# Group 0 of a state-space mixer on one core: the first gate's GEMM ahead of the x transposes, a third convolution buffer, decay weights behind x, one decay factor by VectorE

## The chip, the core and the metric

The kernel runs on one core of one Trainium2 chip. The metric is the device time of one execution in microseconds (us). The time before is the median of three runs, 1901.63 us (1901.63, 1902.76 and 1899.21). A core has a matrix engine (TensorE, PE in the profile), a vector engine (VectorE, DVE), an activation engine (ScalarE, ACT), a general engine (GpSimd, POOL), and SyncE (SP), which here issues the DMA transfers. Each engine works through its own instructions in a fixed order and waits at an instruction whose inputs or buffers are not ready.

## What is computed

The reference is a block of two layers over 512 latent tokens and 256 context tokens of width 1024: attention and a gated FFN, then a bidirectional state-space mixer (SSD) and a gated FFN. The change concerns the mixer only. Cut to what matters:

```python
z, xbc, dt = split(h @ w_in)                 # h: latent tokens, and context tokens apart
xbc = silu(dwconv_centred(xbc, conv_w, conv_b))      # 5 taps along the tokens
x, B, C = split(xbc)                         # 8 groups of 4 heads of 64; B, C: 128 states a group
dt = softplus(dt + dt_bias)
# per direction, in chunks of 128 tokens; acs = cumsum(dt * a) within the chunk
xw     = x * exp(acs_end - acs) * dt         # "decay weights"
states = einsum(B, xw)                       # then a scan over chunks: h = h * exp(acs_end) + states
decay  = exp(where(mask, acs_q - acs_s, -inf))
y      = einsum((C B^T) * decay * dt, x) + (C h) * exp(acs)
out    = rms_norm((y_fwd + y_bwd + d_skip * x) * silu(z)) @ w_out
```

## The kernel before

**Products.** Every GEMM in fp32 is made of three products for each 128x128 weight block: high weights by high activations (L105), high weights by low activations (L106), low weights by high activations (L108). A weight panel of 128x1024 comes by DMA (`wst`, L95), ScalarE casts it to its high part `wh` (L85) and VectorE subtracts to get the low part `wl` (L87). A GEMM over the 512 latent tokens is 8 blocks by 3, so 24 products; with the context tokens 48.

**The mixer (`ssd`, from L1112).** Its 8 groups are processed one after the other. For each group `inproj` (L1257) runs six GEMMs in this order: two halves of x (`xf`), B (`Bf`), C (`Cf`), two gates (`z`). The halves of x and B need latent and context tokens, C and the gates only latent ones. Group 0's two halves of x are computed ahead, together with the norm, so group 0 begins with B and C. An x, B or C result goes through the convolution: `taken` (L1193) copies it from PSUM into one of two padded buffers `raw` on ScalarE (L1197, L1199) and multiplies the centre tap (ScalarE, L1200); `taps` (L1204) adds the other four taps on VectorE (L1205), and ScalarE applies Silu (L1209).

**The core of a group (`core`, L1284)** is a generator with steps between the GEMMs. Step 1 transposes x by 12 TensorE instructions into three PSUM banks (`ps_xt`, L1292), which ScalarE copies out (L1293). Step 2 transposes B (`ps_bt`, L1299, copied at L1300) and multiplies x by the decay weights (`xw`, L1306, VectorE). Step 3 computes C B^T (`ps_cb`, L1337), the first state (`ps_st`, L1318) and the decay matrices `E`: for each of 4 heads and 2 directions d a 128x512 tile is loaded (SP, L1350), masked (GpSimd, L1351), exponentiated by 4 ScalarE instructions (L1355) and multiplied by dt: for d=0 by 4 ScalarE instructions (L1357), for d=1 by one GpSimd instruction (L1359); VectorE adds the two (L1361). Steps 4 to 6 make the later states (VectorE adds `hs`, L1328), the outer part (`ps_yo`, L1383, scaled into `ec` at L1385) and the inner part (`ps_y`, L1392), and VectorE updates `xf` from the PSUM bank (L1395). Those later steps of a group run between the next group's x and B GEMMs, so the next group's x transposes follow right behind `ps_y` and use the PSUM banks that L1385 and L1395 set free.

**Group 0's hooks.** Inside its C GEMM run `turned` (transposes dt and the cumulative sums) and `ends` (L1230): one small matmul for the chunk ends (`ps_end`), eight ScalarE exponentials `dec` (L1238, L1239), and the decay weights `dw`: two subtractions and two multiplications by VectorE and one ScalarE exponential (L1243 to L1249).

**Order and buffers.** A scheduler turns the program into one static order for each engine; `follow` keeps ScalarE's functions in program order, since ScalarE has to load another function table (ACT_TABLE_LOAD) between Exp and Silu. PSUM has two wide buffers (tag S, for GEMMs with context, and before the change for all of them) and four banks of 128x512 (`Bank`). Behind the eight groups `ysplit` (L1429) multiplies each of the 16 gated results by a norm weight and splits them into a high part `hhy` (ScalarE, L1434) and a low part `hly` (VectorE, L1435) for the output projection (`ps_wo`); part of this already runs within group 7.

Of the kernel before, what the change touches and what calls it, by code (L numbers as in the profile page):

```python
# [7 lines left out]
P = 128  # L8
# [9 lines left out]
L = 512  # L18
# [328 lines left out]
def S(g, name):  # L347
    return g.ps.tile([P, 1024], F32, tag="S", bufs=2, name=name)
# [763 lines left out]
def ssd(g, x, norm, wf, close):  # L1112
# [17 lines left out]
    t2 = lambda nm, dt=F32, n=512: g.t3p.tile([P, n], dt, tag="t2", bufs=39, name=nm)  # L1130
    small = lambda nm, shape: g.t3p.tile(shape, F32, name=nm)
    tok = lambda t: slice(t * P + (2 if t >= 4 else 0), (t + 1) * P + (2 if t >= 4 else 0))
    def gemm(w, streams, hooks={}):
        ps = S(g, "ps_in")
        for n, _ in enumerate(gemm_in(g, [(ps, w)], h, (0, L), [[(i, 0, (L, C)[i])] for i in streams])):
            hooks.get(n, lambda: None)()
        return ps[:, :L], ps[:, L:T]


    H2 = 64  # L1140
# [41 lines left out]
            nc.sync.dma_start(dst[rows, :TH], src[H2 * d : H2 * d + 32])  # L1182
            nc.sync.dma_start(dst[rows, TH:], src[H2 * d + 32 : H2 * d + H2, : L - TH])

    raws = [small(f"raw{i}", [P, TW + 4]) for i in range(2)]
    for r in raws:
        for c0 in (0, L + 2, TW + 2):
            nc.vector.memset(r[:, c0 : c0 + 2], 0.0)
# [2 lines left out]
    late = []  # L1191

    def taken(ps, j, both, cv):  # L1193
        raw = raws[raw_n[0] % 2]
        raw_n[0] += 1
        n = TW if both else L
        nc.scalar.copy(raw[:, 2 : 2 + L], ps[0])  # L1197
        if both:
            nc.scalar.copy(raw[:, L + 4 : L + 4 + C], ps[1])  # L1199
        nc.scalar.activation(cv, raw[:, 2 : 2 + n], AF.Identity, scale=par("sw2", j), bias=par("sb", j))  # L1200
        return raw, n, j, cv
# [20 lines left out]
    def turned():  # L1222
        for src, dst in ((acs, acsT), (dt, dtT)):
            pt = Bank(g, "ps_dtT")[:, : nt * H2]
            for t in range(nt // 2):
                nc.tensor.transpose(pt[:, t * P : (t + 1) * P], src[:, t * P : (t + 1) * P], g.ident)
            nc.vector.tensor_copy(dst.rearrange("p (a c) (d h) -> p c d a h", a=2, d=2),
                                  pt.rearrange("p (c d a h) -> p c d a h", c=nt // 2, d=2, a=2))

    def ends():  # L1230
        pe = Bank(g, "ps_end")
        for d, row in ((0, P - 1), (1, 0)):
            nc.tensor.matmul(pe[:, d * nt * 32 : (d + 1) * nt * 32], g.ident[:, row : row + 1].broadcast_to([P, P]),
                             acsT[:, :, d * 32 : (d + 1) * 32], start=True, stop=True)
        pev = pe[:, : nt * H2].rearrange("p (d t h) -> p d t h", d=2, t=nt)
# [8 lines left out]
        follow(g, nc.scalar.activation(dw, dw, AF.Exp))  # L1244
# [12 lines left out]
    def inproj(gi):  # L1257

        G = Group()
        ld = lambda i: load_w(g, I["win"][6 * gi + i])  # L1260
        G.x, ahead = [], {}
        if gi == 0:
            ahead = {2: gemm(ld(2), (1, 0)), 3: gemm(ld(3), (0,), {0: turned, 5: ends})}
        for j in range(2):
            G.x.append(taps(*x0[j]) if gi == 0 else conv(gemm(ld(j), (1, 0)), 2 * gi + j, True, t3(g, "xf")))
            yield G
        for name, i, st in (("B", 2, (1, 0)), ("C", 3, (0,))):
            ps = ahead[i] if ahead else gemm(ld(i), st)
# [15 lines left out]
    def core(gi, G):  # L1284
# [59 lines left out]
        for r in range(4):  # L1344
            hd = 4 * gi + r
            E = []
            for d in range(2):
                row = d * 32 + hd
                e = t2("E")
                nc.sync.dma_start(e, ad[row : row + 1, :].broadcast_to([P, L]))  # L1350
                nc.gpsimd.affine_select(c4(e), c4(e), pattern=[[0, 4], [1 - 2 * d, P]], compare_op=ALU.is_ge,  # L1351
                                        fill=-1e30, base=0, channel_multiplier=2 * d - 1)
                for c in range(4):
                    cs = slice(c * P, (c + 1) * P)
                    follow(g, nc.scalar.activation(e[:, cs], e[:, cs], AF.Exp, bias=nacs[:, c, row : row + 1]))  # L1355
                    if d == 0:
                        nc.scalar.activation(e[:, cs], e[:, cs], AF.Identity, scale=dtT[:, c, row : row + 1])  # L1357
# [3 lines left out]
            nc.vector.tensor_tensor(E[0], E[0], E[1], ALU.add)  # L1361
            W.append(E[0])
# [334 lines left out]
```

## Time and profile before

| what | value |
| --- | --- |
| median of three runs | 1901.63 us |
| time of the profiled execution | 1901.39 us |
| its span in the trace | 1899.6 us |
| mean granted TensorE clock | 0.997 |
| the mixer's group 0, from its C GEMM to group 1's first product | 1014 to 1042 us in the span |

TensorE is busy nearly all of the time, so a change can only win where TensorE waits, and loses where it is made to wait. In the rows shown below, a timeline row gives the start and the duration in us, the engine, line and operation, the tile written and those read, the shape, how many instructions are joined in the row, and, in brackets, the idle time of the engine just before and what ended it. Durations in us are those of all the joined instructions together.

### The profile page before, as it was taken

The page shows a single profiled execution, that of the slowest core. Times are in us where ns is not written, and L with a number is a line of the kernel's source. Part 1 is how long each engine was busy: PE and PEld are TensorE (multiplying, and loading weights), DVE is VectorE, ACT ScalarE, POOL GpSimd, SP SyncE. Part 2 cuts the span into 40 slices and gives each one's busy share as a digit, 9 for nine tenths or more (in the row PEclk, how much of TensorE's full clock was granted, in tenths as well). Part 3 has the DMA queues.
Part 4 walks back from the last instruction along what each step waited for, and adds up shares of the span by engine and source line. Part 5 has one row for each costly group of instructions (what it writes and reads, how often), then busy time and mean ns, then how long its engine had stood idle before and what let it go on. Part 6 is the DMA issues. An engine that isn't in the chain of part 4 may idle for free.

```text
span 1899.6 us, 27442 instructions
## 1 busy us (share of the span) xinstructions
PE 1867.0 (98%) x10794; PEld 1532.9 (81%) x10794; DVE 1336.4 (70%) x2006; ACT 836.0 (44%) x1436; POOL 234.9 (12%) x220
## 2 busy tenths in 40 slices
PE   9999999999999999999998999999999999999999
PEld 7865545689888888888887888888888888888887
DVE  5688989678777777444477777777878576565555
ACT  3655544354222222222256677766667353323331
POOL 2100000030000000000030334443335200000000
PEclk9999999999999999999999999999999999999999
DMA  9223341024443564222223333444344323323232
GB/s 339 68 83 101 100 144 62 1 68 160 152 131 117 174 189 154 67 67 67 67 79 106 104 118 112 122 122 133 112 130 118 98 78 102 101 85 111 89 100 89
DMA packets 73489, 210.02 MB, mean 111 GB/s; under 512 B 8976, under 2 KB 14480, under 8 KB 73232
## 3 DMA queue, kind: packets, MB, share of 16 engines
q1 hardware_dynamic: 73360, 208.26, 35.0%
q8 instruction: 85, 1.39, 0.3%
q14 instruction: 44, 0.36, 0.1%
HBM read 198.79 MB, written 6.82 MB: 108 GB/s over the span
## 4 chain that ended last, share of the span: by engine, by line
PE 81%; DVE 9%; issue 3%; DMA 3%; ACT 3%; POOL 1%; SPq 0%; DVEq 0%; POOLq 0%; ACTq 0%
PE ps_up L105 10%; PE ps_up L106 10%; PE ps_up L108 10%; PE ps_d L105 6%; PE ps_d L108 5%; PE ps_d L106 5%; PE ps_in L106 4%; PE ps_in L108 4%; PE ps_in L105 4%; PE ps_o L799 2%; PE ps_s L835 2%; PE ps_st L1318 2%; PE ps_wo L108 1%; DVE wl L87 1%; PE ps_wo L105 1%
## 5 line engine op out<-in xcount | busy, mean ns | idle before, releaser
L87 DVE TENSOR_TENSOR wl<-wst,wh 128x1024 fp32r<-128x1024 f32 x211 | 263.1, 1247 | 235.4 <-PE ps_up L106 120.7
L85 ACT CAST wh<-wst 128x1024 fp32r<-128x1024 f32 x211 | 221.2, 1049 | 407.1 <-DMA wst<-in_wup 311.1
L106 PE MATMUL ps_up<-hlf,wh 128*128 128x512 f32 x992 | 351.6, 354 | 0.0
L108 PE MATMUL ps_up<-hhf,wl 128*128 128x512 f32 x992 | 351.4, 354 | 0.0
L105 PE MATMUL ps_up<-hhf,wh 128*128 128x512 f32 x992 | 351.2, 355 | 0.0
L105 PEld LDWEIGHTS ps_up<-hhf,wh 128*128 128x128 f32 x992 | 187.5, 189 | 26.2
L106 PEld LDWEIGHTS ps_up<-hlf,wh 128*128 128x128 f32 x992 | 187.6, 189 | 26.0
L108 PEld LDWEIGHTS ps_up<-hhf,wl 128*128 128x128 f32 x992 | 187.5, 189 | 26.1
L105 PE MATMUL ps_in<-hhs,wh 128*128 128x512 f32 (+1 forms) x544 | 199.2, 366 | 0.0
L106 PE MATMUL ps_in<-hls,wh 128*128 128x512 f32 (+1 forms) x544 | 193.9, 356 | 0.0
L108 PE MATMUL ps_in<-hhs,wl 128*128 128x512 f32 (+1 forms) x544 | 193.3, 355 | 0.0
L105 PE MATMUL ps_d<-hdh,wh 128*128 128x512 f32 (+1 forms) x496 | 173.4, 351 | 0.1
L108 PE MATMUL ps_d<-hdh,wl 128*128 128x512 f32 (+1 forms) x496 | 173.4, 350 | 0.0
L106 PE MATMUL ps_d<-hdl,wh 128*128 128x512 f32 (+1 forms) x496 | 172.9, 349 | 0.0
L1015 DVE SCALAR_TENSOR_TENSOR X<-ps_d,mod,X 128x256 f32<-128x256 f32 (+1 forms) x176 | 102.7, 614 | 25.7 <-PE ps_d L108 25.4
L105 PEld LDWEIGHTS ps_in<-hhs,wh 128*128 128x128 f32 x544 | 103.0, 189 | 14.6 <-issue 0.9
L108 PEld LDWEIGHTS ps_in<-hhs,wl 128*128 128x128 f32 x544 | 102.8, 189 | 14.5
L106 PEld LDWEIGHTS ps_in<-hls,wh 128*128 128x128 f32 x544 | 103.1, 189 | 12.9
L106 PEld LDWEIGHTS ps_d<-hdl,wh 128*128 128x128 f32 x496 | 93.2, 188 | 14.4 <-DVE hdl L87 0.2
L108 PEld LDWEIGHTS ps_d<-hdh,wl 128*128 128x128 f32 x496 | 93.2, 188 | 13.1
L105 PEld LDWEIGHTS ps_d<-hdh,wh 128*128 128x128 f32 x496 | 93.0, 188 | 13.1 <-ACT hdh L85 0.3
L838 ACT ACTIVATE pr<-ps_s 128x1024 f32<-128x1024 f32 x56 | 57.2, 1021 | 97.4 <-PE ps_s L837 95.4
(373 smaller groups left out, 3672.5 us busy)
## 6 DMA issues: line engine op xcount, KB each, us to landing
wst<-in_wup SPq DMA_DIRECT2D x88, 512.0 KB, 3.6
wada<-in_adaT SPq DMA_DIRECT2D x56, 512.0 KB, 3.7
wst<-in_win SPq DMA_DIRECT2D x48, 512.0 KB, 3.6
wst<-in_wdown SPq DMA_DIRECT2D x44, 512.0 KB, 3.7
E<-ad SPq DMA_DIRECT2D x64, 256.0 KB, 6.9
wada<-in_adaB SPq DMA_DIRECT2D x24, 512.0 KB, 5.0
ec<-ead SPq DMA_DIRECT2D x64, 128.0 KB, 5.2
wst<-in_wout SPq DMA_DIRECT2D x16, 512.0 KB, 3.7
```

The lines of the kernel that those rows point to most:

```text
L85: keep(nc.scalar.copy(hi, src))
L87: keep(eng.tensor_tensor(lo, src, _r(hi), ALU.subtract))
L105: mm(out, wh, ah, start=first, stop=False)
L106: mm(out, wh, al, start=False, stop=False)
L108: i = mm(out, wl, ah, start=False, stop=last)
L799: nc.tensor.matmul(po[S64[e], :n], v, pr[:, 512 * e + off : 512 * e + off + n], start=first, stop=last)
L835: nc.tensor.matmul(outs[e], a[S64[e], k], b[S64[e], q], start=i == 0, stop=False)
L838: nc.scalar.activation(pr, ps, AF.Exp)
L1015: nc.vector.scalar_tensor_tensor(ap, o[:, c0:c1], gate[:, m, v : v + 1], ap, ALU.mult, ALU.add)
L1318: nc.tensor.matmul(ps[:, d * 256 : (d + 1) * 256], Bt[:, t * P : (t + 1) * P], xw[d][t], start=t == ts[0], stop=t == ts[-1])
```

## The change

Four edits, all in `ssd`. In group 0 the B result is taken right behind its GEMM, and the first gate's GEMM (`first_z`, into a PSUM bank instead of a wide buffer) is issued behind C and ahead of the x transposes. There are three padded `raw` buffers instead of two, in all groups. The decay weights are cut out of `ends` into `weights`, called behind x's taps and Silu. In group 0 the multiplication of the d=0 decay matrices by dt is one VectorE instruction of 128x512 instead of four of ScalarE.

```diff
-    def gemm(w, streams, hooks={}):
-        ps = S(g, "ps_in")
+    def gemm(w, streams, hooks={}, make=S):
+        ps = make(g, "ps_in")
...
-        return ps[:, :L], ps[:, L:T]
+        return ps[:, :L], ps[:, L:T] if make is S else None
...
-    raws = [small(f"raw{i}", [P, TW + 4]) for i in range(2)]
+    raws = [small(f"raw{i}", [P, TW + 4]) for i in range(3)]
...
-        raw = raws[raw_n[0] % 2]
+        raw = raws[raw_n[0] % 3]
...
+    pev = []
+
     def ends():
...
         for i, (tf, tb) in enumerate(steps):
-            follow(g, nc.scalar.activation(dec[:, i, 0], pev[:, 0, tf], AF.Exp))
-            follow(g, nc.scalar.activation(dec[:, i, 1], pev[:, 1, tb], AF.Exp))
-
+            follow(g, nc.scalar.activation(dec[:, i, 0], pev[0][:, 0, tf], AF.Exp))
+            follow(g, nc.scalar.activation(dec[:, i, 1], pev[0][:, 1, tb], AF.Exp))
+
+    def weights():
         for d in range(2):
             hs = slice(d * 32, d * 32 + 32)
-            nc.vector.tensor_tensor(dw[:, :, hs], pev[:, d], acsT[:, :, hs], ALU.subtract)
+            nc.vector.tensor_tensor(dw[:, :, hs], pev[0][:, d], acsT[:, :, hs], ALU.subtract)
         follow(g, nc.scalar.activation(dw, dw, AF.Exp))
         nc.vector.tensor_tensor(dw, dw, dtT, ALU.mult)
...
-        G.x, ahead = [], {}
+        G.x = []
         if gi == 0:
-            ahead = {2: gemm(ld(2), (1, 0)), 3: gemm(ld(3), (0,), {0: turned, 5: ends})}
+            B = taken(gemm(ld(2), (1, 0)), 8 * 2, True, t3(g, "Bf"))
+            Cp = gemm(ld(3), (0,), {0: turned, 5: ends})
+            first_z = gemm(ld(4), (0,), make=Bank)
...
+            if gi == 0:
+                if i == 2:
+                    weights()
+                got = B if i == 2 else taken(Cp, 8 * i, False, t2("Cf"))
+            else:
+                ps = gemm(ld(i), st)
             yield None
-            setattr(G, name, conv(ps, 8 * i + gi, i == 2, t3(g, "Bf") if i == 2 else t2("Cf")))
+            if gi:
+                got = taken(ps, 8 * i + gi, i == 2, t3(g, "Bf") if i == 2 else t2("Cf"))
+            setattr(G, name, taps(*got))
...
-            ps = gemm(ld(4 + j), (0,))
+            ps = first_z if gi == j == 0 else gemm(ld(4 + j), (0,))
...
-                    if d == 0:
+                    if d == 0 and gi:
                         nc.scalar.activation(e[:, cs], e[:, cs], AF.Identity, scale=dtT[:, c, row : row + 1])
-                if d:
-                    nc.gpsimd.tensor_tensor(c4(e), c4(e), dtT[:, :4, row : row + 1].broadcast_to([P, 4, P]), ALU.mult)
+                if d or gi == 0:
+                    (nc.gpsimd if d else nc.vector).tensor_tensor(c4(e), c4(e), dtT[:, :4, row : row + 1].broadcast_to([P, 4, P]), ALU.mult)
```

How it moves the instructions, at three places. The first is TensorE in group 0, from the end of the C GEMM (`hls_7`, `hhs_7` are the last activation blocks of a GEMM, `hhs_0` the first): the difference between the two orders, with the 24 products of the first gate standing between its two pieces.

```order
 L106 MATMUL ps_in<-hls_7_4404,wh 128x512
 L108 MATMUL ps_in<-hhs_7_4403,wl 128x512
-L1292 MATMUL ps_xt<-cst,xf 128x128 x12
 L105 MATMUL ps_in<-hhs_0_4389,wh 128x512
...
 L108 MATMUL ps_in<-hhs_7_4403,wl 128x512
+L1305 MATMUL ps_xt<-cst,xf 128x128 x12
 L105 MATMUL ps_in<-hhs_0_4389,wh 128x512
```

The 12 x transposes stood between C and the first gate; now they stand between the first gate and the second. The B transposes, which stood 5 products into the second gate, now stand 17 products into it. On ScalarE the same stretch, from the cast of group 1's first weight panel to the Silu of B, was before:

```order
L85 CAST wh<-wst 128x1024
L1244 ACTIVATE dw<-dw 128x384
L1209 ACT_TABLE_LOAD
L1209 ACTIVATE xf<-xf 128x770 x2
L1197 COPY raw_9357<-ps_in 128x512
L1199 COPY raw_9357<-ps_in 128x256
L1197 COPY raw_9358<-ps_in 128x512
L1200 ACTIVATE Bf<-raw_9357,par 128x770
L1200 ACTIVATE Cf<-raw_9358,par 128x512
L1293 COPY xt<-ps_xt 128x512 x3
L85 CAST wh<-wst 128x1024
L1209 ACTIVATE Bf<-Bf 128x770
```

and is now:

```order
L85 CAST wh<-wst 128x1024
L1209 ACT_TABLE_LOAD
L1209 ACTIVATE xf<-xf 128x770 x2
L1247 ACT_TABLE_LOAD
L1247 ACTIVATE dw<-dw 128x384
L1197 COPY raw_9357<-ps_in 128x512
L1306 COPY xt<-ps_xt 128x512
L1200 ACTIVATE Cf<-raw_9357,par 128x512
L1306 COPY xt<-ps_xt 128x512 x2
L1209 ACT_TABLE_LOAD
L1209 ACTIVATE Bf<-Bf 128x770
```

B's copy and centre tap have moved ahead of the cast; the exponential of the decay weights has moved behind the Silu of x, between two more table loads. The second place is VectorE at the x transposes of group 3 (groups 5 and 7 read the same), around B's last tap. Before, the update of `xf` from `ps_y` came first and both `ec` behind it:

```order
L87 TENSOR_TENSOR wl<-wst,wh 128x1024
L1205 SCALAR_TENSOR_TENSOR Bf<-raw_9357,par,Bf 128x770
L1395 SCALAR_TENSOR_TENSOR xf<-xf,par,ps_y 128x512
L1385 TENSOR_TENSOR ec<-ec,ps_yo 128x512 x2
L1396 TENSOR_TENSOR xf<-xf,ec 128x512
```

Now one `ec` stands ahead of it:

```order
L87 TENSOR_TENSOR wl<-wst,wh 128x1024
L1205 SCALAR_TENSOR_TENSOR Bf<-raw_9359,par,Bf 128x770
L1398 TENSOR_TENSOR ec<-ec,ps_yo 128x512
L1408 SCALAR_TENSOR_TENSOR xf<-xf,par,ps_y 128x512
L1398 TENSOR_TENSOR ec<-ec,ps_yo 128x512
L1409 TENSOR_TENSOR xf<-xf,ec 128x512
```

On TensorE the three banks of x transposes stood there as 8, four products, 4; they now stand as 8, one product, 4, and the second bank waits for that first `ec`, the third for `xf`. The third place is ScalarE at the end of group 7, ahead of its first decay exponential (`hhy` are the high parts for the output projection). Before:

```order
L1322 COPY hs<-ps_st 128x512
L1434 ACTIVATE hhy_13650<-z,par 128x512
L85 CAST wh<-wst 128x1024
L1434 ACTIVATE hhy_13666<-z,par 128x512
L1355 ACT_TABLE_LOAD
```

Now:

```order
L1335 COPY hs<-ps_st 128x512
L1447 ACTIVATE hhy_13658<-z,par 128x512
L1447 ACTIVATE hhy_13714<-z,par 128x512
L1447 ACTIVATE hhy_13730<-z,par 128x512
L1368 ACT_TABLE_LOAD
```

Eight `hhy` stand ahead of the exponentials now, six before; the two that moved ahead had stood behind the last exponential.

More of the change, by code (lines that the diff above doesn't have):

```diff
@@ L1234, in ends @@
                              acsT[:, :, d * 32 : (d + 1) * 32], start=True, stop=True)
[L1235 removed]
+        pev.append(pe[:, : nt * H2].rearrange("p (d t h) -> p d t h", d=2, t=nt))
         for i, (tf, tb) in enumerate(steps):
[L1238 to L1239 removed]
+            follow(g, nc.scalar.activation(dec[:, i, 0], pev[0][:, 0, tf], AF.Exp))
+            follow(g, nc.scalar.activation(dec[:, i, 1], pev[0][:, 1, tb], AF.Exp))
+    def weights():
         for d in range(2):
             hs = slice(d * 32, d * 32 + 32)
[L1243 removed]
+            nc.vector.tensor_tensor(dw[:, :, hs], pev[0][:, d], acsT[:, :, hs], ALU.subtract)
         follow(g, nc.scalar.activation(dw, dw, AF.Exp))
@@ L1260, in inproj @@
         ld = lambda i: load_w(g, I["win"][6 * gi + i])
-        G.x, ahead = [], {}
+        G.x = []
         if gi == 0:
-            ahead = {2: gemm(ld(2), (1, 0)), 3: gemm(ld(3), (0,), {0: turned, 5: ends})}
+            B = taken(gemm(ld(2), (1, 0)), 8 * 2, True, t3(g, "Bf"))
+            Cp = gemm(ld(3), (0,), {0: turned, 5: ends})
+            first_z = gemm(ld(4), (0,), make=Bank)
         for j in range(2):
-            G.x.append(taps(*x0[j]) if gi == 0 else conv(gemm(ld(j), (1, 0)), 2 * gi + j, True, t3(g, "xf")))
+            G.x.append(taps(*x0[j]) if gi == 0 else
+                       conv(gemm(ld(j), (1, 0)), 2 * gi + j, True, t3(g, "xf")))
             yield G
         for name, i, st in (("B", 2, (1, 0)), ("C", 3, (0,))):
-            ps = ahead[i] if ahead else gemm(ld(i), st)
+            if gi == 0:
[4 more added lines that the diff above has]
+                ps = gemm(ld(i), st)
             yield None
-            setattr(G, name, conv(ps, 8 * i + gi, i == 2, t3(g, "Bf") if i == 2 else t2("Cf")))
+            if gi:
+                got = taken(ps, 8 * i + gi, i == 2, t3(g, "Bf") if i == 2 else t2("Cf"))
+            setattr(G, name, taps(*got))
             yield G
```

## The prediction

> **What bounds the kernel now.** I read the page first, then the list of waits, then the chain of waits and the timelines of the engines around group 0 of the mixer. The page gives the span and the busy times by engine:
>
> ```profile
> span 1899.6 us, 27442 instructions
> PE 1867.0 (98%) x10794; PEld 1532.9 (81%) x10794; DVE 1336.4 (70%) x2006; ACT 836.0 (44%) x1436; POOL 234.9 (12%) x220
> ```
>
> TensorE is idle for 1899.6 - 1867.0 = 32.6 us in all; no other engine can be the bound as a whole, so what counts is which wait of TensorE ends last at a place. The list of waits (us in total, times, longest) has the largest single one in group 0:
>
> ```profile
> PE ps_xt L1292 <- ACT xf L1209: 5.2, 1, 5.2
> PE ps_xt L1292 <- DVE xf L1395: 1.8, 6, 0.5
> ```
>
> The x transposes of group 0 wait 5.22 us for the Silu of x; in the six groups from 2 on they wait 0.3 us on average for a PSUM bank. The chain, in order of time (start, us), tells what the first wait is made of:
>
> ```profile
> 1017.53 3.96 DMA wst<-in_win
> 1021.51 1.05 ACT wh L85
> 1022.56 0.42 ACT dw L1244
> 1023.00 1.28 ACT L1209
> 1024.29 0.85 ACT xf L1209
> ```
>
> ScalarE casts a panel of group 1 that came at 1021.51, does the exponential of the decay weights, loads the Silu table and only then does the Silus. TensorE's timeline of that stretch, from the end of C to group 1's first product:
>
> ```profile
> 1025.19 2.92 PE L1292 MATMUL ps_xt<-cst,xf 128*128 128x128 f32 x12 [5.22 <-ACT xf L1209]
> 1027.77 0.67 PE L105 MATMUL ps_in<-hhs,wh 128*128 128x512 f32 x1
> ...
> 1028.50 0.39 PE L108 MATMUL ps_in<-hhs,wl 128*128 128x512 f32 x1
> ...
> 1034.42 0.39 PE L106 MATMUL ps_in<-hls,wh 128*128 128x512 f32 x1
> ...
> 1034.81 0.88 PE L1299 MATMUL ps_bt<-cst,Bf 128*128 128x128 f32 x6
> ...
> 1035.45 0.48 PE L108 MATMUL ps_in<-hhs,wl 128*128 128x512 f32 x1
> ...
> 1039.87 1.05 PE L1337 MATMUL ps_cb<-Cf,Bf 128*128 128x128 f32 x8
> ...
> 1042.30 0.47 PE L105 MATMUL ps_in<-hhs,wh 128*128 128x256 f32 x1
> ```
>
> C ends at 1025.19 - 5.22 = 1019.97, and nothing runs until 1025.19. Between 1028.50 and 1034.42 stand 26 products, 0.228 us each. The wait costs more than itself, since the clock drops. The windows (span, then PE, PEld, DVE, ACT, POOL, granted clock, DMA share, GB/s) show 0.50 right behind it:
>
> ```profile
> 1025.00:1026.00 1.00, 0.81 (x4) 0.57 (x5) 0.85 (x1) 1.00 (x3) 0.00 (x0) 0.50 0.00 0
> ```
>
> The 12 transposes take 1027.77 - 1025.19 = 2.58 us there. At full clock, in group 1, the same 12 stand in two pieces with the next product behind each:
>
> ```profile
> 1081.47 0.66 PE L1292 MATMUL ps_xt<-cst,xf 128*128 128x128 f32 x4
> 1081.88 0.47 PE L105 MATMUL ps_in<-hhs,wh 128*128 128x512 f32 x1
> ...
> 1082.66 1.20 PE L1292 MATMUL ps_xt<-cst,xf 128*128 128x128 f32 x8
> 1083.61 0.48 PE L105 MATMUL ps_in<-hhs,wh 128*128 128x512 f32 x1
> ```
>
> That is 0.41 + 0.95 = 1.36 us, so the low clock costs 1.2 us.
>
> **The gate's GEMM in the wait.** Its 24 products take 24 x 0.228 = 5.47 us, from 1019.97 to 1025.44. No work is added to TensorE. It can only start at once if its weights are there, which ScalarE's and VectorE's timelines show (casts of both gates' panels, and the low part of one):
>
> ```profile
> 1006.93 2.00 ACT L85 CAST wh<-wst 128x1024 fp32r<-128x1024 f32 x2
> 1008.01 1.23 DVE L87 TENSOR_TENSOR wl<-wst,wh 128x1024 fp32r<-128x1024 f32 x1 [0.18 <-ACT wh L85]
> ```
>
> They lie 10 us ahead. The Silu of x loses the 0.42 us of `dw` ahead of it: cast done at 1022.56, table 1.28, both Silus:
>
> ```profile
> 1024.29 1.58 ACT L1209 ACTIVATE xf<-xf 128x770 f32<-128x770 f32 x2
> 1017.84 3.81 DVE L1205 SCALAR_TENSOR_TENSOR xf<-raw,par,xf 128x770 f32<-128x770 f32 x4
> ```
>
> So x is ready at 1022.56 + 1.28 + 1.58 = 1025.42, just as the gate ends; the taps, 0.95 us each, end near 1023.6 once the decay weights' subtractions stand behind them (1021.65 and two more). The wait of 5.22 us becomes about nothing, the clock stays up, and the transposes end at 1025.44 + 1.36 = 1026.8.
>
> **What is late next.** The 17 products ahead of the B transposes end at 1026.8 + 3.9 = 1030.7. B's Silu now has this ahead of it on ScalarE from 1025.42: a table load, the `dw` exponential, C's copy, a copy of `xt`, C's centre tap, two more copies, a second table load, and its own 0.85 (as x's first Silu in the chain), by these rows:
>
> ```profile
> 1026.51 0.60 ACT L1197 COPY raw<-ps_in 128x512 f32<-128x512 f32 x1
> ...
> 1027.92 0.82 ACT L1200 ACTIVATE Cf<-raw,par 128x512 f32<-128x512 f32 x1
> 1028.63 1.56 ACT L1293 COPY xt<-ps_xt 128x512 f32<-128x512 f32 x3
> ```
>
> 1.28 + 0.42 + 0.60 + 1.56 + 0.82 + 1.28 + 0.85 = 6.8 us, less 0.1 for each of some three overlaps (1027.92 + 0.82 lies 0.11 past the next start): B is ready at 1031.9 to 1032.2, I take 1032.0. TensorE waits 1.3 us there, **a new wait**, where the row at 1034.81 shows next to none now. The bounds: nothing, if the copies overlap more, and 2.8, if C's tap or the copies wait on PSUM as well. Then 0.64 for the transposes (1034.81 to 1035.45), 7 products of 1.6, and 2.43 for `ps_cb` and `ps_st` (1039.87 to 1042.30): group 1 starts at 1036.7 instead of 1042.30. VectorE has to have the weighted x by then:
>
> ```profile
> 1029.01 0.75 DVE L1205 SCALAR_TENSOR_TENSOR Cf<-raw,par,Cf 128x512 f32<-128x512 f32 x1
> ...
> 1035.59 3.02 DVE L1306 TENSOR_TENSOR xw<-xt,dw 128x512 f32<-128x512 f32 x4
> ```
>
> From 1023.6: four taps of B (3.8), two weight subtractions (2.4 by the row at 1008.01), four of C (3.0), about 1.4 for the pieces of `dw` and its neighbours (an estimate), two of the `xw` (1.5): 1035.7, where the second product of the first state would ask for it some 0.3 us earlier. That leaves a gain of **5.3 us** in group 0.
>
> **The edits that I put at nothing.** The d=0 factor takes 16 ScalarE instructions away, and adds four by VectorE:
>
> ```profile
> 1045.19 0.68 ACT L1357 ACTIVATE E<-E,dtT 128x128 f32<-128x128 f32 x2
> 1061.33 0.69 DVE L1361 TENSOR_TENSOR E<-E 128x512 f32<-128x512 f32 x1
> ```
>
> ScalarE saves 16 x 0.29 (start to start) = 4.7 us, VectorE gains 4 x 0.6 to 1.5 us (that sum is slowed beside GpSimd elsewhere in the trace). The products that use these matrices stand behind two GEMMs of group 1, 20 us later, which hides both; with that cover gone it would cost up to 6 us. Three memsets more lie far ahead of group 0. SP now issues the eight loads of the decay matrices behind three weight panels instead of four:
>
> ```profile
> 1036.08 6.38 SPq L1350 DMA_DIRECT2D E<-ad  x8
> ```
>
> The fourth panel, one of group 1 that is wanted three GEMMs (some 30 us) later, is issued some 6 us later for it; that cover hides it, and without it those 6 us would be TensorE's.
>
> **Later groups.** The 5.3 us are a shift, unless a wait changes size. A third `raw` buffer reorders VectorE at the transposes of groups 1 to 7. The rows of group 6, with `xf` ahead of the transposes that it holds up, the second being two `ec`:
>
> ```profile
> 1358.49 0.73 DVE L1395 SCALAR_TENSOR_TENSOR xf<-xf,par,ps_y 128x512 f32<-128x512 f32 x1
> 1359.15 1.27 DVE L1385 TENSOR_TENSOR ec<-ec,ps_yo 128x512 f32<-128x512 f32 x2
> ...
> 1359.28 1.35 PE L1292 MATMUL ps_xt<-cst,xf 128*128 128x128 f32 x8 [0.46 <-DVE xf L1395]
> ```
>
> In groups 3, 5 and 7 one `ec` (0.64) now stands ahead of `xf`, against a weight subtraction less (1.2) since the first tap of x: the bounds are the present wait of 0.3 gone, and 0.6 added, in each; I take +0.2 each, **+0.6**. Group 1, without a wait now, gets the like of the others: **+0.3**. Groups 4 and 6 have their third bank wait for an `ec` alone, and their present waits (0.24 and 0.46) go: **-0.7**. In group 2 the wait for C's Silu goes, as C's taps now begin one place earlier: **-0.6**. At the end of group 7 `ps_y` already waits for a decay exponential:
>
> ```profile
> 1150.38 1.16 PE L1337 MATMUL ps_cb<-Cf,Bf 128*128 128x128 f32 x8 [0.57 <-ACT Cf L1209]
> 1445.79 1.06 PE L1392 MATMUL ps_y<-E,xt 128*64 128x128 f32 x14 [0.90 <-ACT E L1355]
> 1429.73 0.73 ACT L1434 ACTIVATE hhy<-z,par 128x512 fp32r<-128x512 f32 x1
> ```
>
> Two more `hhy` ahead of the exponentials are 2 x 0.62 (the next starts at 1430.35): **+1.2**. Bounds are nothing and 2.2.
>
> **Sum:** -5.3 + 0.6 + 0.3 - 0.7 - 0.6 + 1.2 = -4.5 us. Against the profiled execution (1901.39, of which 1899.6 span; it lies 0.24 under the median of the runs) that gives **1896.9 us**.
>
> **Rivals.** (1) *Nothing given back:* group 0 in full, the later waits of 1.8 and 0.57 gone, and the tail unchanged, because VectorE runs ahead with a third buffer: -5.3 - 2.4 = -7.7, 1893.7. For it speaks the subtraction that left the stretch, against it the rows at 1359, where VectorE works without a gap. (2) *The table switches cost more than their loads.* ScalarE would have to run empty before each; the row at 1023.00 starts 0.02 us after `dw` ends, and Silu 0.01 after the load, against it. If each of the two added switches cost another load's time, B comes 2.6 us later: -1.9, 1899.5. (The Trainium skill, "ScalarE: Activation LUTs", section "What ACT_TABLE_LOAD costs", states a drain of about 1380 ns beside each load of 1283 ns; by it the sum would be -1.7. The trace has the load at 1.28 and no such gap.) (3) *The change doesn't do what it says:* if the gate's panel were the one cast at 1021.51, TensorE would wait 3 to 4 us for it and the rest would follow: -1 to -2, 1900. The casts at 1006.93 speak against it. (4) *Slower:* VectorE late at the second bank in all seven later groups. Without the terms above, group 0 and the tail leave -4.1; a delay d each uses it up at d = 0.6 us, which is one `ec`, and one `ec` and a tap (0.64 + 0.95 = 1.6) in front of it give -4.1 + 11.2 = +7.1, 1908.5. The order has the `ec`, not the tap, and a tap less work in front.
>
> **How the numbers follow.** The forecast, give or take 1.5, has 0.45; rival 1, 0.2; rival 2, 0.1; rival 3, 0.05; a smaller form of rival 4 (0.4 to 0.7 us in each group, 1899 to 1902), 0.13; rival 4 in full, 0.07. What a measurement can tell from no change is about 0.2%, 3.8 us, so faster means below 1897.8. That is some three quarters of the forecast's case and rival 1: 0.53; slower 0.07; the same 0.40. The range reaches to rival 1 and over most of the smaller form of rival 4: 1893.6 to 1901.2.
>
> **What would show it.** No idle time of TensorE between C and the gate, a wait under 0.5 us at the x transposes with the clock at 1.00; a new wait of 1.3 us at the B transposes for ScalarE's Silu; group 1's first product near 1037.0; waits under 0.7 us at the later transposes; 2.1 us at the last `ps_y`. Wrong would be a wait for weights at the gate, a wait of several us at `ps_bt`, `ps_cb` or `ps_st`, or waits over 1 us at the later transposes.

## The result and the profile after

| | before | after |
| --- | --- | --- |
| median of 7 runs each, us | 1899.97 | 1906.87 |
| profiled execution: time, span, us | 1901.39, 1899.6 | 1906.87, 1905.1 |
| A: from `ps_end` to group 1's first product, us | 24.52 | 19.42 |
| B: from there to the start of the last `ps_y` product of group 7, us | 412.9 | 425.9 |

The ratio is 1.0034, with a 95% interval of 1.0023 to 1.0044: slower by 6.5 us by the ratio (the medians differ by 6.9), where the forecast was 4.5 us faster. The two stretches of the table say where. Group 0 won 5.1 us, where 5.3 were forecast; the seven groups behind it, whose code gives the same work, lost 13.0. (What lies ahead of A is 1.7 us shorter after, by one stretch of 3.4 us at half clock that only the trace of before has there; what lies behind B is 0.7 shorter. The start of A lay anywhere between 1014.3 and 1018.8 us in the fourteen kernels profiled here, so I compare stretches and not the span.)

The page of the kernel after, span and busy time by engine:

```profile
span 1905.1 us, 27469 instructions
PE 1868.2 (98%) x10794; PEld 1533.7 (81%) x10794; DVE 1349.4 (71%) x2013; ACT 834.8 (44%) x1422; POOL 227.3 (12%) x220
```

TensorE does the same 10794 matmuls. ScalarE has 14 instructions fewer (16 gone, two table loads come), VectorE seven more (four products, three memsets). Nothing here looks like a loss; TensorE's idle time has grown from 32.6 to 36.9 us. The list of waits of the kernel after (engine, tile, who ended the wait; us in all, times, longest) has its new entries on top:

```profile
PE ps_xt L1305 <- DVE ec L1398: 9.0, 6, 3.0
PE ps_xt L1305 <- DVE xf L1408: 1.9, 1, 1.9
...
PE ps_bt L1312 <- ACT Bf L1209: 1.2, 1, 1.2
```

The 5.2 us for the Silu of x are gone, and 1.2 us at B's transposes have come. But the later x transposes, which waited 1.8 us in all for a PSUM bank, now wait 10.9. By group, 1 to 7: 0.17, 1.90, 1.22, 1.87, 1.71, 2.98, 1.09. With the smaller waits at `ps_cb` and `ps_y` that is 12.5 us against 3.2 in stretch B, 9.2 of the 13.0 lost. Some 3.4 more is the clock behind two of those waits, by windows of the kernel after (span, then PE, PEld, DVE, ACT, POOL, granted clock, DMA share, GB/s):

```profile
1135.00:1137.00 2.00, 2.00 (x6) 1.58 (x5) 0.68 (x1) 1.01 (x2) 1.28 (x1) 0.51 0.00 0
1137.00:1139.00 2.00, 2.00 (x7) 1.56 (x6) 0.70 (x2) 1.23 (x2) 0.45 (x1) 0.64 0.00 0
...
1363.00:1365.00 2.00, 1.88 (x8) 1.59 (x9) 1.32 (x3) 2.00 (x4) 0.55 (x1) 0.68 0.00 0
1365.00:1367.00 2.00, 2.00 (x6) 1.51 (x6) 1.20 (x2) 0.34 (x1) 0.73 (x1) 0.50 0.00 0
```

Each window of 2 us loses 2 x (1 - clock): 0.98 + 0.72 behind the wait of group 2, 0.64 + 1.0 behind that of group 6 (and 0.06 in the next window, at 0.97): 1.7 us each time. In stretch B of before the clock does not fall.

**Group 0** reads as forecast. TensorE's timeline of the kernel after (start, duration, operation, shape, idle time before it):

```profile
1016.04 0.81 PE L1235 MATMUL ps_end<-acsT,cst 128*128 128x192 f32 x4
...
1023.54 1.47 PE L1305 MATMUL ps_xt<-cst,xf 128*128 128x128 f32 x12
...
1030.13 0.88 PE L1312 MATMUL ps_bt<-cst,Bf 128*128 128x128 f32 x6 [1.22 <-ACT Bf L1209]
...
1033.74 2.08 PE L1331 MATMUL ps_st<-xw,Bt 128*128 128x256 f32 x8 [0.22 <-DVE xw L1319]
1035.46 0.47 PE L105 MATMUL ps_in<-hhs,wh 128*128 128x256 f32 x1
```

The transposes have no wait in brackets and last 1.47 us where they lasted 2.92.

**Later groups.** VectorE has one long stretch of work, from the first later state (which needs the first part of `ps_st`) to the row that frees the waited bank of x transposes. TensorE's timeline of group 6, before:

```profile
1326.60 2.75 PE L1318 MATMUL ps_st<-xw,Bt 128*128 128x256 f32 x12
```

and after:

```profile
1327.46 2.75 PE L1331 MATMUL ps_st<-xw,Bt 128*128 128x256 f32 x12
...
1363.12 0.66 PE L1305 MATMUL ps_xt<-cst,xf 128*128 128x128 f32 x4 [2.98 <-DVE ec L1398]
```

Counted from the start of `ps_st`, TensorE is ready for that bank at 1359.28 - 0.46 - 1326.60 = 32.2 us before (by the row of 1359.28 in the prediction, where it is the second of the three banks) and at 1363.12 - 2.98 - 1327.46 = 32.7 after, where it is the third; it gets it at 32.7 before and 35.7 after. VectorE is 3 us late. Its stretch begins, before, with

```profile
1327.73 0.69 DVE L1328 TENSOR_TENSOR hs<-hs,ps_st 128x512 f32<-128x512 f32 x1 [8.08 <-PE ps_st L1318]
1328.34 0.68 DVE L1361 TENSOR_TENSOR E<-E 128x512 f32<-128x512 f32 x1
```

and after it begins and ends with

```profile
1327.48 1.42 DVE L87 TENSOR_TENSOR wl<-wst,wh 128x1024 fp32r<-128x1024 f32 x1 [7.10 <-PE ps_in L106]
1328.83 0.68 DVE L1341 TENSOR_TENSOR hs<-hs,ps_st 128x512 f32<-128x512 f32 x1
1331.62 1.10 DVE L1374 TENSOR_TENSOR E<-E 128x512 f32<-128x512 f32 x1 [2.12 <-POOL E L1372]
...
1362.38 0.68 DVE L1398 TENSOR_TENSOR ec<-ec,ps_yo 128x512 f32<-128x512 f32 x1
```

A weight subtraction of 1.42 us now stands ahead of the first state, and the sum of the decay matrices waits 2.12 us for GpSimd's factor, which was ready before. The decay matrices come late from their loads on. SP's loads and GpSimd's first factor for this stretch, before:

```profile
1310.08 5.75 SPq L1350 DMA_DIRECT2D E<-ad  x8
1324.11 1.05 POOL L1359 TENSOR_TENSOR E<-E,dtT 128x512 f32<-128x512 f32 x1 [0.60 <-ACT E L1355]
```

and after:

```profile
1317.12 5.68 SPq L1363 DMA_DIRECT2D E<-ad  x8
1330.55 1.05 POOL L1372 TENSOR_TENSOR E<-E,dtT 128x512 f32<-128x512 f32 x1
```

SP begins the loads 16.5 us ahead of `ps_st` before and 10.3 after, and the factor, done 1.4 us ahead of `ps_st` before, is done 4.1 behind its start. It is the same in all six stretches that end at the transposes of groups 2 to 7: the loads stand on SP behind one weight panel more than before, and that panel waits for a buffer until a GEMM ends.

The windows over the whole stretch, before:

```profile
1326.60:1359.20 32.60, 32.22 (x205) 27.93 (x203) 28.70 (x33) 20.64 (x46) 9.24 (x7) 1.00 0.26 78
1161.40:1194.10 32.70, 32.70 (x209) 28.38 (x207) 28.45 (x32) 21.22 (x47) 9.25 (x7) 1.00 0.23 67
```

and after (the first of each is group 6, the second group 3):

```profile
1327.40:1363.10 35.70, 32.74 (x209) 28.25 (x208) 31.77 (x34) 23.07 (x52) 14.87 (x13) 1.00 0.31 91
1157.50:1190.10 32.60, 31.38 (x201) 27.30 (x201) 29.57 (x33) 22.19 (x53) 13.43 (x11) 1.00 0.34 94
```

VectorE, the third busy column, is busy 28.70 of 32.60 us in group 6 before: 88%, in a kernel where its share of the span is 70%. After it needs 31.77. That is one subtraction more (34 instructions against 33) and slower ones, beside a GpSimd that has 13 instructions there in place of 7: four of its masks and the first factor, among others, now fall into the stretch. The 3.9 us of idle time are the same in sum. Group 3 is of another kind. VectorE is busier (29.57 against 28.45 in windows of nearly the same length) and yet not later, but TensorE asks earlier. TensorE's timeline before:

```profile
1161.44 2.75 PE L1318 MATMUL ps_st<-xw,Bt 128*128 128x256 f32 x12
...
1192.10 0.66 PE L1292 MATMUL ps_xt<-cst,xf 128*128 128x128 f32 x4
...
1193.52 0.60 PE L1292 MATMUL ps_xt<-cst,xf 128*128 128x128 f32 x4
1194.35 0.66 PE L1292 MATMUL ps_xt<-cst,xf 128*128 128x128 f32 x4 [0.23 <-DVE xf L1395]
```

and after:

```profile
1157.56 2.75 PE L1331 MATMUL ps_st<-xw,Bt 128*128 128x256 f32 x12
...
1190.10 0.66 PE L1305 MATMUL ps_xt<-cst,xf 128*128 128x128 f32 x4 [1.22 <-DVE ec L1398]
```

The waited bank comes free 32.9 us behind `ps_st` before and 32.5 after. TensorE asked for it at 32.7, as the third bank of its transposes; it now asks at 31.3, since it is the second. By these rows the old order of the transposes was 4, four products, 8, and not the 8, four products, 4 that the section on the change has; so the second bank, asked for at 32.1 before, is now asked for four products sooner.

How late the bank is goes by when the sum of the decay matrices can start. In groups 3, 5 and 7 of the kernel after and of two of the runs below (`e4` and `e6`), TensorE and VectorE have the same rows in the same order up to the bank. The sum starts 2.5 to 3.8 us behind `ps_st` in these nine stretches, always after a wait for GpSimd's factor, the bank comes free 29.7 to 29.8 us behind the sum, and TensorE's wait goes from 0.98 to 2.21 us with it. With one order the wait of a group thus differs by up to 1.2 us from trace to trace; smaller differences between single groups say nothing below.

### The profile page after: what moved, and what is told of

Read it like the earlier page. It is cut to its first block, busy times and chain, and to the rows that moved or that the text cites. A ratio compares the mean times of both kernels' runs of the same rounds, so it can differ in the third digit from the quotient of the medians.

```text
span 1905.1 us, 27469 instructions
## 1 busy us (share of the span) xinstructions
PE 1868.2 (98%) x10794; PEld 1533.7 (81%) x10794; DVE 1349.4 (71%) x2013; ACT 834.8 (44%) x1422; POOL 227.3 (12%) x220
## 4 chain that ended last, share of the span: by engine, by line
PE 72%; DVE 13%; issue 5%; ACT 4%; DMA 3%; POOL 2%; SPq 1%; DVEq 0%; POOLq 0%; ACTq 0%
PE ps_up L105 10%; PE ps_up L106 10%; PE ps_up L108 10%; PE ps_d L105 6%; PE ps_d L108 5%; PE ps_d L106 5%; DVE xf L1205 2%; PE ps_o L799 2%; PE ps_in L106 2%; PE ps_in L108 2%; PE ps_in L105 2%; PE ps_s L835 2%; DVE wl L87 1%; PE ps_wo L105 1%; PE ps_wo L108 1%
```

## The experiments

The theory was that VectorE's order in the later groups is what costs, and the first question which of the edits changes it, since none touches those groups but the third buffer. Rivals were that buffer, and the work that VectorE gained.

**The factor back on ScalarE** (`e1`), the rest of the change kept:

```diff
-                    if d == 0 and gi:
+                    if d == 0:
...
-                if d or gi == 0:
-                    (nc.gpsimd if d else nc.vector).tensor_tensor(c4(e), c4(e), dtT[:, :4, row : row + 1].broadcast_to([P, 4, P]), ALU.mult)
+                if d:
+                    nc.gpsimd.tensor_tensor(c4(e), c4(e), dtT[:, :4, row : row + 1].broadcast_to([P, 4, P]), ALU.mult)
```

> The changed kernel with group 0's d=0 factor back on ScalarE; gate, third buffer and split weights stay. Its order of VectorE in groups 2 to 7 is that of before again (the xf update ahead of both ec at B's last tap). Theory (the factor's move changes the scheduler's order of the later groups, and that order costs the time): the waits at the later x transposes fall from 10.9 us to about 2, group 0 keeps its gain, 1893 to 1897 us. Rival A (VectorE is the bound of groups 2 to 7 at any order, so a gain of TensorE in group 0 is given back there): 1902 to 1908. Rival B (the third buffer reorders the later groups, as the prediction had it): unchanged, 1905 to 1908.

**The factor alone** (`e2`): the kernel before, with only those lines of the change.

> The kernel of before with only the d=0 factor of group 0 moved to VectorE. Theory (order): waits of 8 to 11 us at the later x transposes where before has 1.8, 1907 to 1911 us. Rival A (TensorE arriving earlier is the cause): TensorE does not arrive earlier here, so 1899 to 1901. Rival B (third buffer): 1899 to 1901. The prediction's price for the edit itself was nothing.

**The third buffer alone** (`e3`), on the kernel before:

```diff
-    raws = [small(f"raw{i}", [P, TW + 4]) for i in range(2)]
+    raws = [small(f"raw{i}", [P, TW + 4]) for i in range(3)]
...
-        raw = raws[raw_n[0] % 2]
+        raw = raws[raw_n[0] % 3]
```

> The kernel of before with only the third raw buffer. Its order of VectorE in the later groups is that of before. Theory (order by the factor): 1899 to 1901 us, waits at the later transposes about 2. Rival B (the third buffer): 8 us slower or more, about 1908.

**The factor on GpSimd** (`e4`): the change, with the product on GpSimd in place of VectorE.

```diff
-                    (nc.gpsimd if d else nc.vector).tensor_tensor(c4(e), c4(e), dtT[:, :4, row : row + 1].broadcast_to([P, 4, P]), ALU.mult)
+                    nc.gpsimd.tensor_tensor(c4(e), c4(e), dtT[:, :4, row : row + 1].broadcast_to([P, 4, P]), ALU.mult)
```

> The changed kernel with the four d=0 factors of group 0 on GpSimd instead of VectorE: no added VectorE work, but ScalarE is as free as in the changed kernel, and the later groups have the changed kernel's order. Theory (the order, not the work of the four instructions): 1904 to 1909 us, waits at the later transposes near 10. Rival C (the four VectorE instructions push VectorE back, and it never recovers): waits near 2, 1894 to 1898.

Measured (the medians of before that the ratios go by lie between 1899.75 and 1900.9; A and B are the stretches of the table above):

| | median us | ratio to before | A | B |
| --- | --- | --- | --- | --- |
| e1, factor back | 1896.67 | 0.9985 [0.9976, 0.9994] | 19.68 | 412.9 |
| e2, factor alone | 1912.76 | 1.0066 [1.0053, 1.0078] | 25.12 | 424.5 |
| e3, buffer alone | 1892.81 | 0.9964 [0.9952, 0.9977] | 19.05 | 412.6 |
| e4, factor on GpSimd | 1908.02 | 1.0039 [1.0026, 1.0053] | 19.23 | 426.3 |

The first line of the waits at the x transposes, of e1:

```profile
PE ps_xt L1305 <- DVE xf L1408: 1.5, 6, 0.4
```

of e2:

```profile
PE ps_xt L1292 <- DVE ec L1385: 11.9, 7, 2.7
```

and of e4:

```profile
PE ps_xt L1305 <- DVE ec L1398: 10.9, 6, 2.8
```

The later loss comes and goes with the factor, by itself 11.6 us in B, more than I expected; and it stays when VectorE does not do the factor at all. So the third buffer is not its cause, and VectorE's four products are not either. What e2, e4 and the change have in common is that ScalarE no longer has those 16 instructions in group 0.

The third buffer alone was expected to change next to nothing. It made the fastest kernel of the study. Its waits at the x transposes:

```profile
PE ps_xt L1292 <- DVE xf L1395: 2.0, 6, 0.5
...
PE ps_xt L1292 <- ACT xf L1209: 0.9, 1, 0.9
```

The wait of 5.2 us has shrunk to 0.9, with the gate's code where it was. ScalarE's timeline gives the reason: in e3 B's result is copied out of its wide PSUM buffer, into the third `raw`, at

```profile
1011.70 0.57 ACT L1197 COPY raw<-ps_in 128x512 f32<-128x512 f32 x1
1012.17 0.37 ACT L1199 COPY raw<-ps_in 128x256 f32<-128x256 f32 x1
```

and in the kernel before only behind x's Silus, when x's taps had let go of a `raw`:

```profile
1025.78 0.57 ACT L1197 COPY raw<-ps_in 128x512 f32<-128x512 f32 x1
1026.25 0.37 ACT L1199 COPY raw<-ps_in 128x256 f32<-128x256 f32 x1
```

With the wide buffer free 14 us earlier, the scheduler itself puts 18 of the gate's 24 products ahead of the x transposes.

**The same work with the instructions back** (`e5`) tells apart the order and the work. ScalarE gets 16 multiplications by 1.0, in place, where its factor was; VectorE still does the factor:

```diff
                     if d == 0 and gi:
                         nc.scalar.activation(e[:, cs], e[:, cs], AF.Identity, scale=dtT[:, c, row : row + 1])
+                    elif d == 0:
+                        nc.scalar.activation(e[:, cs], e[:, cs], AF.Identity, scale=1.0)
```

> The changed kernel, with VectorE still multiplying the d=0 matrices of group 0 by dt, and 16 ScalarE instructions (a multiplication by 1.0 in place) put where before had the factor. VectorE's work is that of the changed kernel in every group; its order from group 3 on is that of before but for one row in group 6. Theory (the order alone costs the time): waits at the later x transposes about 2 us, stretch from group 1 to the last inner product as in e1 (412 us against 425 in the changed kernel), 1894 to 1899 us. Rival C (VectorE's added work): waits near 10, 1904 to 1909.

Measured: 1895.62, ratio 0.9973 [0.9963, 0.9983], B 413.5. The waits at the x transposes of e5:

```profile
PE ps_xt L1305 <- DVE xf L1410: 2.7, 6, 1.2
```

More work than the change, on VectorE the same, and 11.3 us faster. Sixteen ScalarE instructions that compute nothing bring back the old order of TensorE, GpSimd and (but for one row in group 6) VectorE in the stretches of groups 3 to 7, and with it the loads 16.5 us ahead of `ps_st`. Group 2 keeps another order, its loads begin 10.0 us ahead, and it is the one with the wait of 1.2 us. The loss is the static order that the scheduler chose.

**What in that order costs.** The second question was whether one move would mend it. The update of `xf` ahead of both `ec` (`e6`) tried the row that the transposes wait for; the weight subtractions of the gates behind the last later state (`e7`) tried the subtraction ahead of the first state; the first later state ahead of the sums of the decay matrices (`e12`) tried GpSimd's factor in front of the states.

```diff
+            pos = []
...
-                late.append(nc.vector.tensor_tensor(ec[d], ec[d], po, ALU.mult))
-            nc.gpsimd.tensor_tensor(ec[0], ec[0], ec[1], ALU.add)
+                pos.append(po)
...
+            for d in range(2):
+                late.append(nc.vector.tensor_tensor(ec[d], ec[d], pos[d], ALU.mult))
+            nc.gpsimd.tensor_tensor(ec[0], ec[0], ec[1], ALU.add)
```

> The changed kernel with the update of xf written ahead of both ec; that changes VectorE's order only at B's last tap in groups 4 and 6 (update, then both ec, as before had it there). The prediction's step (the row that frees the bank sets the wait): the waits of groups 4 and 6, 1.87 and 2.98 us now, fall to 0.2 to 0.6. Theory (what stands ahead of VectorE's stretch, from the first later state on, sets it): they stay within 0.7 us of what they are, and the time within 2 us of the changed kernel, 1905 to 1909.

`e7` (`behind` adds an order between two instructions, `last_hs` is the last later state):

```diff
-            ps = first_z if gi == j == 0 else gemm(ld(4 + j), (0,))
+            if gi:
+                wz = ld(4 + j)
+                behind(g.last_wl, last_hs[0])
+                ps = gemm(wz, (0,))
+            else:
+                ps = first_z if j == 0 else gemm(ld(4 + j), (0,))
```

> The changed kernel with the low parts of the gates' weight panels bound behind the last later state of the group before, so that none stands ahead of the first state on VectorE (one fewer there in groups 2 to 7; group 2's order becomes that of before). Theory (what stands ahead of the first later state delays the whole stretch): the wait of group 2 falls from 1.9 to about 0.2, those of groups 3 to 7 by 0.5 to 1.2 each, 1901 to 1904 us. If only the row that frees the bank matters, waits of groups 3 to 7 stay and the time is 1905 to 1907.

`e12`:

```diff
-            nc.vector.tensor_tensor(E[0], E[0], E[1], ALU.add)
-            W.append(E[0])
+            W.append(E)
...
-        for i in range(1, 4):
+        state(1, xw)
+        i1 = last_hs[0]
+        for n, E in enumerate(W):
+            behind(nc.vector.tensor_tensor(E[0], E[0], E[1], ALU.add), i1)
+            W[n] = E[0]
+        for i in range(2, 4):
```

> The changed kernel with the sums of the two decay matrices bound behind the first later state, so that VectorE no longer waits for GpSimd's factor ahead of it in groups 3, 5 and 7 (there the first later state starts 3.6 to 4.3 us behind TensorE's product now, 1.1 in groups 2, 4 and 6, whose order stays). Theory (each delay ahead of or within VectorE's stretch is passed on): in groups 3, 5 and 7 the first state starts about 1.1 us behind, and the waits there (1.22, 1.71, 1.09) fall below 0.7; those of groups 2, 4 and 6 stay between 1.3 and 3; 1902 to 1905 us. Rival (the wait for GpSimd is only moved behind the state, and the stretch ends as late): waits of groups 3, 5 and 7 stay over 1 us, 1905 to 1908.

Measured: e6 1908.37, 1.0040 [1.0026, 1.0053]; e7 1915.19, 1.0078 [1.0064, 1.0093]; e12 1912.25, 1.0066 [1.0049, 1.0083]. None mended anything, and e7 and e12 are slower than either of their expectations. In e6 the bank came with the other row and as late (waits of 2.42 and 2.19 us in groups 4 and 6). In e7 the stretch holds as many subtractions as in the change, but the one that stood at its head, while VectorE waited for GpSimd's factor anyway, now comes behind the states; the waits grew to 3.11 to 4.65 us in groups 3 to 7: a miss by sign. In e12 the first state did start 1.2 to 1.3 us behind `ps_st` in groups 3, 5 and 7, and the waits there stayed at 1.99, 1.20 and 1.40. In all three the loads of the decay matrices still begin 10 to 11 us ahead of `ps_st`, and the first sum starts 2.3 to 4.3 us behind it. That late start is common to every stretch of groups 2 to 7 with a wait of 0.98 us or more, in e2 and e4 too; in all others the loads begin 16.5 us ahead or sooner, and the wait is 0.87 or less. No run moved the loads alone, so that they are the cause within the order is read from the traces and not tested.

**Is the stretch without slack?** (`e9`) The kernel before, with one weight subtraction of 128x1024 done a second time in groups 2 to 7 (`last_st` is the staged panel):

```diff
+            wz = ld(4 + j)
+            if gi >= 2 and j:
+                nc.vector.tensor_tensor(wz[1], g.last_st, _r(wz[0]), ALU.subtract)
-            ps = gemm(ld(4 + j), (0,))
+            ps = gemm(wz, (0,))
```

> The kernel of before with one VectorE subtraction of 128x1024 (1.2 us) repeated without effect in each group from 2 on. The scheduler puts it ahead of the row that frees the bank in groups 3, 5 and 7, and behind that row in groups 2, 4 and 6. Theory (between the later states and the freed bank VectorE has no slack in any order, although it is busy 70% of the span): waits of 1.2 to 2 us at the x transposes of groups 3, 5 and 7 (0.2 to 0.4 before), and under 0.7 in groups 2, 4 and 6; 1903 to 1906 us. If VectorE had slack there: no wait over 0.6 us, 1899 to 1902 us.

Measured: 1912.01, 1.0061 [1.0048, 1.0074]. Six times 1.2 us on an engine that idles 30% of the span cost 12 us, 2 a group, more than either theory gave. The waits of e9:

```profile
PE ps_cb L1341 <- ACT Cf L1210: 9.0, 6, 2.7
...
PE ps_xt L1296 <- DVE ec L1389: 2.0, 3, 0.8
PE ps_xt L1296 <- DVE xf L1399: 1.9, 3, 0.9
```

The transposes wait 2 us more than before, `ps_cb` 8.4 more: VectorE is behind there too, with C's taps, which ScalarE's Silu and then TensorE wait for. That fits a stretch without slack, and the shortage runs on past the x transposes. But the scheduler moved other rows as well (in groups 3, 5 and 7 one `ec` stands ahead of `xf`, and the taps of C alternate with the products of the weighted x), so the 12 us are the price of the work and of these moves together.

**What the parts of the change are worth without the new order.** The gate's GEMM ahead and the third buffer, without the factor and the weights (`e8`); the gate alone (`e10`); the weights behind x alone (`e11`), each on the kernel before, with the change's own lines. For e8 the difference to the change is, beside the lines of e1:

```diff
-    def weights():
...
-                if i == 2:
-                    weights()
```

> Before with the first gate ahead of the x transposes and the third buffer; decay weights and factor as before. VectorE's order of the later groups is that of before. Against e3 (third buffer alone, where 18 of the gate's 24 products already stand ahead of the transposes) the wait of 0.9 us at the x transposes goes; against e1 two table loads ahead of B's Silu go: no wait over 0.5 us in group 0, 1891 to 1894 us. If the split of the decay weights is worth its place, it is slower than e1 (1896.7).

`e10`:

```diff
+            first_z = gemm(ld(4), (0,), make=Bank)
...
-            ps = gemm(ld(4 + j), (0,))
+            ps = first_z if gi == j == 0 else gemm(ld(4 + j), (0,))
```

> The kernel of before with only the first gate's GEMM ahead of the x transposes. Order of VectorE from group 3 on as before. The prediction's step for the gate: the wait of 5.2 us falls to under 1 us, waits at the B transposes appear (B's convolution still waits for x's buffers, so B comes later than in the changed kernel, 1 to 4 us), 1894 to 1898 us.

`e11`:

```diff
+    def weights():
...
+            if ahead and i == 2:
+                weights()
```

> The kernel of before with only the decay weights behind x's taps and Silu. Order of VectorE in the later groups as before. By the rows, x's Silu comes 0.4 us sooner and two table loads stand ahead of B's Silu, which had 2.8 us of idle time ahead of it: the wait at the x transposes 4.7 to 5.0 us, 1899 to 1902 us.

Measured: e8 1893.16, 0.9966 [0.9953, 0.9979]; e10 1898.62 and e11 1898.48, both 0.9994 [0.9985, 1.0003]. With the gate ahead the wait at x is 0.16 to 0.17 us, with the buffer or without. A new wait of 1.1 us (e8) and 1.4 (e10) at B's transposes comes with it, which e8 was not expected to have: it isn't the weights' exponential and its table loads that make B late. e10 falls short of what was expected. A is only 2.9 us shorter than before (21.58), and behind B it is 3.2 us longer, 1.7 of them a stretch at half clock. Two waits at the output projection have come there:

```profile
PE ps_wo L106 <- DVE yl L1436: 1.0, 1, 1.0
...
PE ps_wo L105 <- ACT yh L1435: 0.5, 1, 0.5
```

Here, too, the order moved far from the edit; e1 has the same two waits, 1.5 us, and a tail longer by 3.3. The weights alone shorten the wait at x from 5.2 to 4.7 us, and are no gain that can be measured. The fastest kernels are e3 and e8, 0.35% under before and not to be told apart: the buffer alone does as much as the gate and the buffer.

## Why the prediction was wrong

- **The gate in the wait: right.** No wait at the x transposes, the clock at full, A shorter by 5.1 us where 5.3 were forecast. The new wait at B was forecast at 1.3 and is 1.22, the one for the weighted x at 0.3 and is 0.22.
- **"Later groups", the price of the new order: the step that failed.** The terms +0.6, +0.3, -0.7 and -0.6, together -0.4 us, stood for what took 9.0 us in waits at the transposes and `ps_cb`, and 3.4 in clock: wrong in size and, for some groups, in sign. Groups 3, 5 and 7 were put at +0.2 each and took +1.0, +1.5 and +0.7; groups 4 and 6 at -0.7 together and took +1.6 and +2.5; group 2 took +1.7 more at its transposes. I compared the few rows ahead of the transposes, "one `ec` against a weight subtraction less", and took the rest of VectorE's stretch as it was. At the start of the stretch, 30 us ahead, a subtraction had come in all six groups, and VectorE then waited for GpSimd's factor, whose loads SP began 6 us later than before; in groups 3, 5 and 7 TensorE's turn had come one bank earlier. None of this was in the sum. SP's order I read for group 0 alone, where the loads had moved the other way.
- **"The edits that I put at nothing": half right.** What ScalarE saves and VectorE gains is indeed hidden, as e5 shows with the same factor on VectorE and more on ScalarE. But the edit isn't only its instructions. It changed the order of all later groups, and e1 against the change puts that at 10.2 us in the medians (13.0 in B).
- **"A third `raw` buffer reorders VectorE": wrong cause.** e3 has the buffer and, in the later groups, no more than 2.0 us of waits at the x transposes. That the order had moved was in view; the edit that moved it was guessed.
- **The tail** was put at +1.2 and took 0.25: `ps_y` waits 0.84 us for ScalarE, where it waited 0.90, and 0.31 for VectorE. The wait for C's Silu did not go; it is 0.36 in place of 0.57, in another group.
- **The rivals.** The fourth is what happened, nearly: VectorE is late in six of the seven groups (group 1 waits 0.17), at the second bank in groups 3, 5 and 7 and at the third in 2, 4 and 6. Its sum, -4.1 + 7d, with the measured d = (10.9 - 1.8) / 7 = 1.3 us gives +5.0; the profiled executions differ by 5.5. That these agree so well is in part luck, as the sum has no term for the clock and has the tail at +1.2. I gave it 0.07 in full because "the order has the `ec`, not the tap, and a tap less work in front", which is the same reading of too few rows. The second rival, slow table switches, did not come. ScalarE's timeline of the kernel after has the first added load and the exponential 0.01 us behind its end:

```profile
1023.47 1.28 ACT L1247 ACT_TABLE_LOAD   x1
1024.76 0.53 ACT L1247 ACTIVATE dw<-dw 128x384 f32<-128x384 f32 x1
...
1029.24 0.85 ACT L1209 ACTIVATE Bf<-Bf 128x770 f32<-128x770 f32 x1
```

What stays open: by which of its rules the scheduler takes another order for groups 2 to 7 when 16 instructions of group 0 go. No run tests that. And the share of each part of the new order (the later loads and GpSimd's factor, the extra subtraction, TensorE's earlier turn) was not isolated: no run moved the loads, and the runs that moved one part moved others with it.

## What to carry to other kernels

An engine's share of the span says nothing of its slack: measure from the event that starts its stretch to the row that the bound engine waits for, and set that against when the bound engine asks for it (here 32.7 to 32.9 us against 32.2 to 32.7, on an engine that is 70% busy). Then see what the engine itself waits for at the start of the stretch, back to the loads. Where a scheduler fixes the order, an edit costs what its new order costs, in places that the edit doesn't touch; compare the whole stretch on every engine and on the queue of the loads, and hold each edit alone against before. A buffer more that lets a PSUM tile go early can bring the reorder that one would write by hand, and 0.36% with two changed lines.

## What was not expected of the hardware

The granted clock fell to 0.51 behind TensorE's wait of 1.90 us in group 2 and to 0.50 behind the 2.98 in group 6, but not behind the 1.87 of group 4, by the window of the kernel after right behind that one:

```profile
1248.00:1250.00 2.00, 1.84 (x10) 1.63 (x11) 1.35 (x3) 2.00 (x4) 0.57 (x1) 1.00 0.00 0
```

So waits of one length have two prices here, 1.9 us and about 3.6: the clock stays low for 3.4 us, which is 1.7 us lost, or does not fall. (The Trainium skill, "TensorE: Matmul & The Clock Gate", section "What's actually happening", has the clock go to half after at least one idle window of about 3.4 us, in windows that run freely. Half the clock agrees; 1.90 us of idle time that bring it do not, and a free-running window would fit that like waits fare unlike, which no run here shows.)
